# A one-layer decoder trunk on one core: residual strips turned once per feature pair, two weight sums moved to VectorE, and five joins of the last two token tiles as TensorE products

## The chip, the cores and the metric

The kernel runs on 1 core of one Trainium2 chip. The metric is the device time of one execution in microseconds; of several runs the median counts. Engines: TensorE (PE; its weight loads are listed as PEld), VectorE (DVE), ScalarE (ACT), GpSimd (POOL), and SyncE (SP), which issues most of the DMAs.

## The reference, cut to what matters

512 tokens of 2048 features, fp32, go through one layer. The change touches the feed-forward part and the end:

```python
h = h + concat([out_a, out_b]) @ w_o             # mixer, not touched
u = rmsnorm(h, ln_ffn)
gate = causal_dwconv(u @ w_gate, conv_f_w, conv_f_b)     # 2048 -> 6144, 3 taps
h = h + (gelu(gate) * (u @ w_up)) @ w_down
u = rmsnorm(h, ln_ple)
e = sigmoid(u @ w_ple_gate) * (p @ w_ple_proj)
h = h + rmsnorm(e, ln_ple_post)
out = rmsnorm(h, ln_final)
```

## The kernel before, in words

Every matrix product is done in three terms: each operand is split into a rounded high part and a low part (ScalarE writes the high part, line 138, VectorE the low part, line 139), and TensorE adds high x high, high x low and low x high. Weights come by DMA, are split by `wfill_`, and up to three split weights stand ready ahead of TensorE (`LOOK`, `HL`).

Phase 1 (to about 900 us) is the mixer. Phase 2 has four stages.

**Gate stage (about 905 to 1820 us).** `w_gate` and `w_up` are multiplied in blocks of 128 output features, with the recursion for 2x2 blocks that needs seven products instead of eight. `gate_order` lists the units: for each n from 0 to 47 (n // 2 is the pair of feature blocks, n % 2 the matrix, gate or up) the seven products `q5 p1 p4 p6 p7 p2 p3`, 336 in all, each 24 matmuls of 256 columns (lines 1302 to 1304). `unit` does one of them. Its weight operand is a sum of weight quarters, made by `gate_unit`: `q5` loads two quarters and VectorE adds them (line 1143) into the buffer `"s"`; for `p6` and `p3` GpSimd then adds another quarter into the same buffer with an accumulating DMA (line 1160). The first and last n do the `p6` sum on VectorE. The buffers are x0 to x3 for even n and x4 to x7 for odd n. The units start `p1 p4 p2` of n = 0, `p1` of n = 1, `q5 p7 p6` of n = 0, then `q5 p4` of n = 1, `p3` of n = 0, `p6 p7 p2` of n = 1, `q5` of n = 2.

After `p3` of an even n the convolution and GELU write the tile c in x9 (`conv`, lines 1346 to 1352); after `p3` of the odd n the product of both is taken (line 1433), and every second pair is spilled to DRAM (`spill`, with four subtractions on VectorE).

Beside it the residual h, 16 strips of 128 features x 512 tokens in DRAM (`hd`), is turned to token order (`hx`), for use after 2100 us: `turn` transposes 32x32 blocks on VectorE (line 1404) and stores them with four DMAs in pieces of 128 bytes (line 1407); the strip is loaded into the tile `acc` (named row in the trace) by line 1414. The program places a turn at every 18th unit.

Instructions of this stage are ordered by a scheduler: each goes when its operands are ready in the scheduler's own model, the higher priority first; weight loads and splits have a raised priority. On each engine, and in the SP queue, the order is then fixed, and each instruction waits for its turn.

**Down stage and embedding gate (about 1820 to 2497 us).** Not touched by the change.

**The end.** The last 256 gate columns are done per token tile (tt = 0 to 3, 128 tokens each), in the order written by hand on TensorE, VectorE, ScalarE and GpSimd. For each tile: 48 matmuls of 256 columns; a tanh (line 1699) and a chain of small VectorE and ScalarE operations (lines 1700 to 1705); `rstd` (line 1636) with a power on GpSimd (line 1623) gives the scale r; `joined` computes e r + h for a block of 512 columns (line 1650, four blocks a tile); `rfin` (lines 1641 to 1644) with a second power on GpSimd gives the last scale; `final` multiplies a block by it (ScalarE line 1655, VectorE line 1657) and stores it (line 1658). The join of block 3 of a tile and its four `final` blocks come after the next tile's chain.

Of the kernel before, what the change touches and what calls it, by code (L numbers as in the profile page):

```python
# [6 lines left out]
AF = mybir.ActivationFunctionType  # L7
# [6 lines left out]
KT = D // 128  # L14
# [6 lines left out]
NF = FF // 128  # L21
# [69 lines left out]
class Builder:  # L91
# [1039 lines left out]
    def gate_unit(self, n, u):  # L1131
        nc, p, w = self.nc, n // 2, n % 2
        par = 4 * w
        src = lambda i, j: self.A["wgu"][2 * p + i, w, j]
        buf = lambda i: self.t(self.bp, "x%d" % (par + i), (128, 8, 128), bufs=1)

        def load(k, i, j):
            t = buf(k)
            nc.sync.dma_start(t, src(i, j))
            return t  # L1140
        def add(o, a, b):
            with self.tc.high_priority(offset=-W['offw'] if n < 1 else 0):
                nc.vector.tensor_tensor(o, a, b, ALU.add)
            return o
        g = self.gw.setdefault(n, {})
        if u == "q5":
            g[21], g[22], g["s"] = load(0, 1, 0), load(1, 1, 1), buf(3)
            return add(g["s"], g[21], g[22])
        if u == "p1":
            g[11] = load(2, 0, 0)  # L1150
            return g[11]
        if u == "p4":
            return g[22]
        if u == "p7":
            if n < 2:
                g[11] = load(2, 0, 0)
            return add(g[21], g[21], g[11])
        if u == "p6" and n in (0, NF - 1):
            return add(g["s"], g["s"], g[11])
        nc.gpsimd.dma_start(g["s"], src(0, 0 if u == "p6" else 1), accum_op=ALU.add)  # L1160
        return g["s"]

# [68 lines left out]
    def phase2(self):  # L1231
        nc, A, k2 = self.nc, self.A, self.k2
        V, SC, G, TE = nc.vector, nc.scalar, nc.gpsimd, nc.tensor
# [5 lines left out]
        acc = self.t(self.cp, "row", (128, S + 2), bufs=1)[:, 0:S]  # L1239
        self.LOOK = 3  # L1240
        hd = [self.dp.tile([128, 2, S], F32, name="hd%d" % i) for i in range(8)]
# [52 lines left out]
        B = lambda n, shape=(128, 2, S), dt=F32: self.t(self.bp, "x%d" % n, shape, dt, bufs=1)  # L1294
# [106 lines left out]
        hx = [self.dp.tile([S, 512], F32, name="hx%d" % i) for i in range(4)]  # L1401

        def turn(m):
            V.transpose(acc, acc)
            for a in range(4):
                f = m % 4 * 128 + 32 * a
                nc.sync.dma_start(hx[m // 4][:, f:f + 32].rearrange("(b i) j -> i b j", i=32),
                                  acc[32 * a:32 * a + 32].rearrange("i (b j) -> i b j", j=32))

        raw, c = [], None  # L1410
        for k, (n, u) in enumerate(self.gate_order()):
            m = k // 18 - 1
            if 0 <= m < KT and k % 18 == 6:
                nc.sync.dma_start(acc, hd[m // 2][:, m % 2])
            if 0 <= m < KT and k % 18 == 10:
                turn(m)
            for m in late.get((n, u), ()):
                squares(m)
            unit(n, u)
            if n == 1 and u == "p6":  # L1420
                self.rstd_bcast(acc, D, RMS_EPS, k2, rs, rt)
                c = B(9)
                conv(0, o, c)
            if u != "p3":
                continue
            p, o = n // 2, G_.pop(n)["out"]
            if n == 0:
                continue
            if n % 2 == 0:
                c = B(9)  # L1430
                conv(p, o, c)
                continue
            V.tensor_tensor(o, o, c, ALU.mult)
            raw.append(o)
            if p % 2 == 1:
                spill(p // 2, raw)
                raw = []
# [3 lines left out]
        h3 = [PT[{0: 5, 1: 3, 2: 6, 3: 4}[2 * (tt // 2) + cb // 2]][cb % 2][:, tt % 2] for tt in range(4) for cb in range(4)]  # L1441
# [58 lines left out]
        def small(n):  # L1500
            nonlocal at
            at += n
            return row[:, at - n:at]
# [47 lines left out]
        for cb in (0, 2, 1, 3):  # L1551
# [5 lines left out]
            if cb == 3:  # L1557
                for k in range(2):
                    r = T("e", 2, (128, 2, S))[:, 0]
# [18 lines left out]
        MU, AD = ALU.mult, ALU.add  # L1578
        et = [self.slot(n) for n in (39, 15, 40, 41, 42, 43, 0, 1)]
        e = [et[i % 8][:, i // 8] for i in range(16)]  # L1580
# [66 lines left out]
        def joined(tt, r, cbs):  # L1647
            for cb in cbs:
                ix = tt * 4 + cb
                V.scalar_tensor_tensor(e[ix], e[ix], r, h3[ix], MU, AD)  # L1650

        def final(tt, r, cb, act=True):
            ix = tt * 4 + cb
            if act:
                SC.activation(e[ix], e[ix], AF.Copy, scale=r)
            else:
                V.tensor_scalar(e[ix], e[ix], r, None, MU)
            nc.sync.dma_start(A["out"][tt * 128:(tt + 1) * 128, cb * S:(cb + 1) * S], e[ix])

        for cb in range(4):  # L1660
# [8 lines left out]
            n, w = (8, 512) if cb < 3 else (4, 256)  # L1669
# [18 lines left out]
        with self.tc.manual_schedule(engines={ET.PE, ET.DVE, ET.Activation, ET.Pool}):  # L1688
            for tt in range(4):
                pg = {tt: self.mm()[:, 0:256]}  # L1690
                for u in range(5):
                    if u == len(us):
                        us.append(self.wnext())
                    k = 2 * u if u < 2 else 4 * u - 4
                    gate(pg, [tt], us[u:u + 1], range(k, KT), u == 0, u == 4)

                sg, ee, x = T("e", 2, (128, 2, S))[:, 0], T("e", 2, (128, 2, S))[:, 0], e[tt * 4 + 3][:, last]
                n5 = slice(tt * 5 + 4, tt * 5 + 5)
                SC.activation(sg[:, last], pg[tt], AF.Tanh, scale=rsh[:, tt:tt + 1])
                V.scalar_tensor_tensor(ee[:, last], sg[:, last], 1.0, pp[tt][:, last], AD, MU)  # L1700
                SC.activation(ee[:, last], ee[:, last], AF.Square, accum_out=ss[:, n5])
                V.scalar_tensor_tensor(x, sg[:, last], 1.0, pp[tt][:, 0:256], AD, MU)
                SC.activation(sg[:, 0:256], x, AF.Square, accum_out=sg2[:, n5])
                V.scalar_tensor_tensor(ee[:, 0:256], hq[tt // 2][:, tt % 2, 0:256], 2.0, x, MU, MU, accum_out=sb[:, n5])
                V.tensor_tensor(x, x, gfin[3][:, last], MU)
                rn = rstd(tt)
                if tt:

                    joined(tt - 1, r, (3,))
                    for cb in range(4):  # L1710
                        final(tt - 1, rf, cb)
                r = rn
                joined(tt, r, (0,))
                rf = rfin(tt, r)
                joined(tt, r, (1, 2))
            joined(3, r, (3,))
            for cb in range(4):
                final(3, rf, cb, cb < 3)

# [64 lines left out]
```

## Time and profile before

| what | us |
|---|---|
| median of 3 runs | 2527.17 |
| lowest and highest run | 2523.64, 2529.2 |
| the profiled execution | 2528.72 |
| its span, first to last instruction | 2526.9 |
| TensorE matmul busy in the span | 2473.3 |
| VectorE busy in the span | 1903.1 |

The profile is of one execution. A row of a timeline has start, duration, engine, line, operation and tiles, and in brackets the idle time of the engine before it with what ended it. In the chain of waits each piece is followed back from the end to what released it.

### The profile page before, as it was taken

How to read it: one execution, taken by the hardware profiler on the slowest of the kernel's cores; microseconds unless marked ns; L12 is line 12 of the kernel's file. 1: busy time of each engine (PE TensorE's matmuls, PEld its weight loads, DVE VectorE, ACT ScalarE, POOL GpSimd, SP SyncE). 2: the span in 40 equal slices, each digit the busy share in tenths (PEclk: the TensorE clock that was granted, in tenths of full speed). 3: DMA queues.
4: the chain of work that ended last, by engine and by line, in shares of the span. 5: the costliest groups of instructions: out<-in, count | busy, mean ns of one | idle time of the engine just before them, and what ended most of it. 6: DMA issues, size and time to landing. Idle time of an engine off the chain costs nothing.

```text
span 2526.9 us, 51719 instructions
## 1 busy us (share of the span) xinstructions
PE 2473.3 (98%) x21858; PEld 2182.3 (86%) x21858; DVE 1903.1 (75%) x2626; ACT 1250.0 (49%) x1735; POOL 220.3 (9%) x244
## 2 busy tenths in 40 slices
PE   9989999999999989999999999999999999999997
PEld 8867777777777889999999999999988888888887
DVE  5855775776585879878988888888877787896457
ACT  6563654556442545434444444444466454535345
POOL 0000100101031000000000000000000000000001
PEclk9999999999999999999999999999999999999998
DMA  7222222222342568888877777776788686853333
GB/s 260 89 78 63 88 77 65 88 81 68 102 131 93 161 198 218 203 212 221 211 196 176 204 194 193 203 196 176 213 250 234 172 264 188 254 130 117 100 92 109
DMA packets 168570, 402.17 MB, mean 159 GB/s; under 512 B 48529, under 2 KB 60817, under 8 KB 168337
## 3 DMA queue, kind: packets, MB, share of 16 engines
q1 hardware_dynamic: 133744, 307.62, 36.9%
q0 software_dynamic: 19872, 72.36, 17.3%
q10 hardware_dynamic: 14720, 18.88, 2.2%
q8 instruction: 171, 2.80, 0.5%
q14 instruction: 63, 0.51, 0.1%
HBM read 358.16 MB, written 40.63 MB: 158 GB/s over the span
## 4 chain that ended last, share of the span: by engine, by line
PE 60%; DVE 5%; DMA 3%; issue 2%; ACT 1%; POOL 0%; SPq 0%; POOLq 0%; ACTq 0%; DVEq 0%
PE mm L1304 7%; PE mm L1303 7%; PE mm L1302 7%; PE mm L1448 6%; PE mm L1447 6%; PE mm L1451 6%; PE wk L1302 3%; PE wk L1303 3%; PE wk L1304 3%; PE mm L1590 2%; PE mm L1591 2%; PE mm L1592 2%; PE mm L173 2%; PE mm L175 2%; PE mm L177 2%
## 5 line engine op out<-in xcount | busy, mean ns | idle before, releaser
L138 ACT ACTIVATE whi<-x 128x1024 fp32r<-128x1024 f32 x332 | 351.1, 1061 | 450.5 <-PE mm L1303 181.2
L139 DVE TENSOR_TENSOR wlo<-x,whi 128x1024 fp32r<-128x1024 f32 x332 | 404.7, 1219 | 120.4 <-ACT whi L138 116.5
L1302 PE MATMUL mm<-s,whi 128*128 128x256 f32 x1432 | 398.0, 278 | 4.5 <-ACT whi L138 3.6
L1304 PE MATMUL mm<-s,wlo 128*128 128x256 f32 x1432 | 398.3, 278 | 3.8 <-DVE wlo L139 3.7
L1303 PE MATMUL mm<-s,whi 128*128 128x256 f32 x1432 | 397.9, 278 | 0.0
L138 ACT ACTIVATE whi<-wraw 128x1024 fp32r<-128x1024 f32 (+1 forms) x223 | 227.0, 1018 | 341.7 <-PE mm L175 165.3
L139 DVE TENSOR_TENSOR wlo<-wraw,whi 128x1024 fp32r<-128x1024 f32 (+1 forms) x223 | 269.4, 1208 | 132.3 <-ACT whi L138 130.3
L173 PE MATMUL mm<-x,whi 128*128 128x512 f32 x832 | 332.5, 400 | 1.5 <-DVE hT L468 0.9
L177 PE MATMUL mm<-x,wlo 128*128 128x512 f32 x832 | 332.1, 399 | 0.0
L175 PE MATMUL mm<-x,whi 128*128 128x512 f32 x832 | 330.5, 397 | 0.0
L1302 PEld LDWEIGHTS mm<-s,whi 128*128 128x128 f32 x1432 | 270.6, 189 | 5.0 <-ACT whi L138 3.8
L1304 PEld LDWEIGHTS mm<-s,wlo 128*128 128x128 f32 x1432 | 270.0, 189 | 4.7 <-DVE wlo L139 4.7
L1303 PEld LDWEIGHTS mm<-s,whi 128*128 128x128 f32 x1432 | 270.1, 189 | 0.2
L1448 PE MATMUL mm<-whi,s 128*128 128x512 f32 x680 | 265.4, 390 | 0.9 <-DVE s L157 0.9
L1447 PE MATMUL mm<-whi,s 128*128 128x512 f32 x680 | 265.6, 391 | 0.0
L173 PEld LDWEIGHTS mm<-x,whi 128*128 128x128 f32 x832 | 157.1, 189 | 37.1 <-issue 2.7
L177 PEld LDWEIGHTS mm<-x,wlo 128*128 128x128 f32 x832 | 156.9, 189 | 34.0 <-issue 1.9
L175 PEld LDWEIGHTS mm<-x,whi 128*128 128x128 f32 x832 | 157.1, 189 | 33.7 <-issue 1.8
L1451 PE MATMUL mm<-wlo,s 128*128 128x512 f32 x680 | 181.3, 390 | 0.0
L1302 PE MATMUL wk<-s,whi 128*128 128x256 f32 x584 | 162.5, 278 | 2.0 <-ACT whi L138 2.0
L1304 PE MATMUL wk<-s,wlo 128*128 128x256 f32 x584 | 162.4, 278 | 0.4 <-DVE wlo L139 0.4
L1160 POOL DMA_DIRECT2D x<-wgu x94 | 82.7, 880 | 913.5 <-DVE wlo L139 663.9
(579 smaller groups left out, 5386.2 us busy)
## 6 DMA issues: line engine op xcount, KB each, us to landing
x<-wgu SPq DMA_DIRECT2D x144, 512.0 KB, 4.4
x<-wgu POOLq DMA_DIRECT2D x94, 512.0 KB, 5.7
wraw<-wz SPq DMA_DIRECT2D x80, 512.0 KB, 3.5
x<-wd SPq DMA_DIRECT2D x52, 512.0 KB, 6.0
wraw<-wgu SPq DMA_DIRECT2D x51, 512.0 KB, 4.6
x<-wd POOLq DMA_DIRECT2D x44, 512.0 KB, 6.0
wraw<-wpg SPq DMA_DIRECT2D x31, 512.0 KB, 3.5
rd<-x SPq DMA_DIRECT2D x24, 512.0 KB, 4.7
```

The lines of the kernel that those rows point to most:

```text
L138: nc.scalar.activation(hi, raw, AF.Copy)
L139: nc.vector.tensor_tensor(lo, raw, hi.bitcast(F32), ALU.subtract)
L173: nc.tensor.matmul(ps, hi[:, k, :], xh, start=first and i == 0, stop=False)
L175: nc.tensor.matmul(ps, hi[:, k, :], xl, start=False, stop=False)
L177: nc.tensor.matmul(ps, lo[:, k, :], xh, start=False, stop=last and i == n - 1)
L1160: nc.gpsimd.dma_start(g["s"], src(0, 0 if u == "p6" else 1), accum_op=ALU.add)
L1302: TE.matmul(ps, wh[:, k, :], xh, start=k == 0, stop=False)
L1303: TE.matmul(ps, wh[:, k, :], xl, start=False, stop=False)
L1304: TE.matmul(ps, wl[:, k, :], xh, start=False, stop=k == 7)
L1447: TE.matmul(ps, x[0][:, k, ts_(tt)], w[0][:, k, :], start=first and k == 0, stop=False)
L1448: TE.matmul(ps, x[1][:, k, ts_(tt)], w[0][:, k, :], start=False, stop=False)
L1451: TE.matmul(ps, x[0][:, k, ts_(tt)], w[1][:, k, :], start=False, stop=last and k == 1)
```

## The change

In the gate stage `p3` of n = 0 and `p6` of n = 1 no longer use an accumulating DMA: SP loads the quarter and VectorE adds it. `p7` of n = 1 uses the quarter that `p6` has loaded.

A turn now writes its transpose into a tile of x9, where the convolution's result lay, and not into `acc`; the next strip is loaded into `acc` right after the transpose. Turns come after the product of an odd n (n = 3, 5, ... 33), one per pair, instead of every 18th unit.

At the end, the joins of blocks 1, 2 and 3 of tile 2 and of blocks 1 and 2 of tile 3 become two TensorE products each, added up in PSUM: identity x h, and diag(r) x e, where diag(r) is the identity scaled by VectorE. Their `final` reads PSUM. The `final` of tile 3 runs in the order 0, 3, 1, 2, with 0 and 1 on ScalarE and 3 and 2 on VectorE, instead of 0, 1, 2 on ScalarE and 3 on VectorE.

```diff
@@ gate_unit
         if u == "p7":
-            if n < 2:
+            if n < 1:
                 g[11] = load(2, 0, 0)
             return add(g[21], g[21], g[11])
-        if u == "p6" and n in (0, NF - 1):
+        if u == "p6" and n in (0, 1, NF - 1):
+            if n == 1:
+                g[11] = load(2, 0, 0)
             return add(g["s"], g["s"], g[11])
+        if u == "p3" and n == 0:
+            return add(g["s"], g["s"], load(1, 0, 1))
         nc.gpsimd.dma_start(g["s"], src(0, 0 if u == "p6" else 1), accum_op=ALU.add)
@@ phase2, gate stage
         def turn(m):
-            V.transpose(acc, acc)
+            h = B(9)[:, 0]
+            V.transpose(h, acc)
+            if m + 1 < KT:
+                nc.sync.dma_start(acc, hd[(m + 1) // 2][:, (m + 1) % 2])
             for a in range(4):
                 f = m % 4 * 128 + 32 * a
                 nc.sync.dma_start(hx[m // 4][:, f:f + 32].rearrange("(b i) j -> i b j", i=32),
-                                  acc[32 * a:32 * a + 32].rearrange("i (b j) -> i b j", j=32))
+                                  h[32 * a:32 * a + 32].rearrange("i (b j) -> i b j", j=32))
...
-        for k, (n, u) in enumerate(self.gate_order()):
-            m = k // 18 - 1
-            if 0 <= m < KT and k % 18 == 6:
-                nc.sync.dma_start(acc, hd[m // 2][:, m % 2])
-            if 0 <= m < KT and k % 18 == 10:
-                turn(m)
+        for n, u in self.gate_order():
...
             if n == 1 and u == "p6":
                 self.rstd_bcast(acc, D, RMS_EPS, k2, rs, rt)
+                nc.sync.dma_start(acc, hd[0][:, 0])
...
             V.tensor_tensor(o, o, c, ALU.mult)
             raw.append(o)
+            if 0 < p <= KT:
+                turn(p - 1)
@@ phase2, the end
+        def onto(tt, cbs, stream):
+            for cb in cbs:
+                ix = tt * 4 + cb
+                if stream:
+                    sums[ix] = self.mm()
+                    TE.matmul(sums[ix], self.K("ident"), h3[ix], start=True, stop=False)
+                else:
+                    TE.matmul(sums[ix], diag[tt], e[ix], start=False, stop=True)
...
+                if tt == 3:
+                    onto(2, (1, 2, 3), True)
+                    onto(2, (1, 2, 3), False)
+                    onto(3, (1, 2), True)
...
-                    joined(tt - 1, r, (3,))
+                    if tt < 3:
+                        joined(tt - 1, r, (3,))
                     for cb in range(4):
                         final(tt - 1, rf, cb)
                 r = rn
+                if tt >= 2:
+                    V.tensor_scalar(diag[tt], self.K("ident"), r, None, MU)
                 joined(tt, r, (0,))
                 rf = rfin(tt, r)
-                joined(tt, r, (1, 2))
+                if tt < 2:
+                    joined(tt, r, (1, 2))
             joined(3, r, (3,))
-            for cb in range(4):
-                final(3, rf, cb, cb < 3)
+            onto(3, (1, 2), False)
+            for cb in (0, 3, 1, 2):
+                final(3, rf, cb, cb < 2)
```

More of the change, by code (lines that the diff above doesn't have):

```diff
@@ L1650, in joined @@
                 V.scalar_tensor_tensor(e[ix], e[ix], r, h3[ix], MU, AD)
+        sums = {}
+        diag = {tt: small(128) for tt in (2, 3)}
+        def onto(tt, cbs, stream):
[6 more added lines that the diff above has]
+                    TE.matmul(sums[ix], diag[tt], e[ix], start=False, stop=True)
         def final(tt, r, cb, act=True):
             ix = tt * 4 + cb
+            x = sums.get(ix, e[ix])
             if act:
-                SC.activation(e[ix], e[ix], AF.Copy, scale=r)
+                SC.activation(e[ix], x, AF.Copy, scale=r)
             else:
-                V.tensor_scalar(e[ix], e[ix], r, None, MU)
+                V.tensor_scalar(e[ix], x, r, None, MU)
             nc.sync.dma_start(A["out"][tt * 128:(tt + 1) * 128, cb * S:(cb + 1) * S], e[ix])
```

## The prediction

> **What bounds the kernel now.** I read the page's engine rows first, then windows by stage, then TensorE's waits, then the chain of waits and the timelines where windows lose matmuls, last the timelines of the end. All rows are of the one profiled execution.
>
> ```profile
> PE 2473.3 (98%) x21858; PEld 2182.3 (86%) x21858; DVE 1903.1 (75%) x2626; ACT 1250.0 (49%) x1735; POOL 220.3 (9%) x244
> ```
>
> TensorE is busy 98% of the span, so a change pays only where TensorE stands or runs slowly, and after its last product. Windows show where. Columns: window, length, then busy time and count of TensorE's matmuls and weight loads, VectorE, ScalarE, GpSimd; last the granted clock, DMA share and GB/s.
>
> ```profile
> 920.00:930.00 10.00, 10.00 (x89) 10.00 (x88) 3.20 (x4) 2.84 (x5) 1.86 (x2) 0.99 0.65 168
> 930.00:950.00 20.00, 15.58 (x112) 15.09 (x112) 15.98 (x21) 7.78 (x10) 3.88 (x4) 0.83 0.65 144
> 1000.00:1080.00 80.00, 80.00 (x708) 80.00 (x707) 66.05 (x77) 36.20 (x39) 7.01 (x8) 1.00 0.88 217
> 1080.00:1245.00 165.00, 161.68 (x1375) 160.57 (x1374) 138.40 (x160) 70.22 (x78) 14.92 (x17) 1.00 0.87 219
> 1180.00:1240.00 60.00, 60.00 (x512) 60.00 (x511) 53.38 (x62) 29.38 (x33) 5.24 (x6) 1.00 0.84 199
> 1300.00:1400.00 100.00, 100.00 (x885) 100.00 (x884) 85.60 (x96) 44.88 (x49) 9.30 (x11) 1.00 0.76 199
> ```
>
> Undisturbed (1300 to 1400) the gate stage does 885 matmuls in 100 us, one per 0.113 us. Between 930 and 950 it does 112 where 177 fit: 65 x 0.113 = 7.3 us lost. Between 1080 and 1245 it does 1375 where 1460 fit: 85 x 0.113 = 9.6 us lost, although busy time lacks only 3.3 us. The rest is a slower pace at full clock: 512 in 60 us is 8.53 per us, against 8.85 between 1000 and 1080 (3.6% less). It follows the stalls and lasts long. Who stalls TensorE between 860 and 1250 (total, times, longest):
>
> ```profile
> PE mm L1304 <- DVE wlo L139: 3.7, 3, 1.8
> PE mm L1302 <- ACT whi L138: 3.6, 1, 3.6
> ```
>
> It waits for split weights. The chain of waits near 930, then GpSimd's timeline, one row each of ScalarE's and TensorE's, and two of VectorE's:
>
> ```profile
> 923.65 1.23 DVE x L139
> 924.88 0.61 DVE row L1279
> 925.49 3.70 issue
> 929.19 5.49 DMA x<-wgu
> ```
> ```profile
> 919.96 1.08 POOL L1160 DMA_DIRECT2D x<-wgu  x1 [93.57 <-DVE wlo L139]
> 929.19 0.89 POOL L1160 DMA_DIRECT2D x<-wgu  x1 [8.14 <-issue]
> ```
> ```profile
> 929.01 1.06 ACT L138 ACTIVATE whi<-x 128x1024 fp32r<-128x1024 f32 x1 [4.60 <-DMA x<-wgu]
> ```
> ```profile
> 937.77 0.58 PE L1302 MATMUL mm<-s,whi 128*128 128x256 f32 x1 [3.58 <-ACT whi L138]
> ```
> ```profile
> 918.42 2.35 DVE L139 TENSOR_TENSOR wlo<-x,whi 128x1024 fp32r<-128x1024 f32 x2
> ...
> 923.65 1.23 DVE L139 TENSOR_TENSOR x<-x,x 128x1024 fp32r<-128x1024 f32 x1 [2.28 <-ACT x L138]
> ```
>
> GpSimd issues two accumulating DMAs, in the code those of (0, "p3") and (1, "p6"). The first starts at 919.96 and ScalarE gets its data at 929.01, some 9 us later. The second's destination was split by 924.9, but it starts at 929.19, when the first had landed, and takes 5.49. TensorE stands for it from 934.2 to 937.8.
>
> The other kind of stall, again by the chain of waits, and VectorE's group of the transposes between 960 and 1200 (the last numbers are its idle time before them and what ended it):
>
> ```profile
> 1070.75 4.42 DMA hx<-row
> ...
> 1075.31 7.67 DMA row<-hd
> ```
> ```profile
> L1404 DVE STREAM_TRANSPOSE row<-row 128x512 f32<-128x512 f32 x15 | 10.6, 710 | 27.6 <-DMA row<-hd 13.9 <-issue 9.1 <-DMA x<-wgu 4.5
> ```
>
> The transposed strip is stored, only then is the next strip loaded into the same tile, and VectorE, which issues in order, stands at the transpose with the next weight split behind it: 27.6 us before 15 transposes.
>
> The end, by the timelines of TensorE, VectorE, GpSimd, ScalarE and SP:
>
> ```profile
> 2510.05 0.28 PE L1592 MATMUL mm<-whi,s 128*128 128x256 f32 x1
> ```
> ```profile
> 2512.18 0.75 DVE L1650 SCALAR_TENSOR_TENSOR s<-s,row,x 128x512 f32<-128x512 f32 x1 [0.43 <-POOL row L1623]
> ...
> 2513.68 0.74 DVE L1650 SCALAR_TENSOR_TENSOR x<-x,row,x 128x512 f32<-128x512 f32 x1
> 2514.34 0.74 DVE L1650 SCALAR_TENSOR_TENSOR s<-s,row,x 128x512 f32<-128x512 f32 x1
> 2515.00 0.42 DVE L1700 SCALAR_TENSOR_TENSOR e<-e,x 128x256 f32<-128x256 f32 x1
> ...
> 2518.03 0.75 DVE L1650 SCALAR_TENSOR_TENSOR s<-s,row,x 128x512 f32<-128x512 f32 x1 [0.43 <-POOL row L1623]
> ```
> ```profile
> 2519.68 0.98 POOL L1623 TENSOR_TENSOR row<-row,mhalf 128x1 f32<-128x1 f32 x1 [1.69 <-DVE row L1644]
> ```
> ```profile
> 2520.70 1.34 ACT L1655 ACTIVATE s<-s,row 128x512 f32<-128x512 f32 x2 [1.89 <-POOL row L1623]
> 2521.94 0.71 ACT L1655 ACTIVATE x<-x,row 128x512 f32<-128x512 f32 x1
> ```
>
> TensorE is done at 2510.3, and the last 16 us are VectorE, GpSimd and ScalarE. VectorE is late: it begins token tile 3's own chain (L1700) only at 2515.00.
>
> **The change, part by part.** Durations for it: VectorE's adds, a scaled 128x128, a full-precision product (two records) from the timeline, and the landing of the strips' stores.
>
> ```profile
> L1143 DVE TENSOR_TENSOR x<-x,x x98: 1210/1219/1227, 903.0 to 1813.3; 128x1024 f32<-128x1024 f32 x98
> L741 DVE TENSOR_SCALAR bdr<-con,par x8: 246/286/287, 25.2 to 661.5; 128x128 f32<-128x128 f32 x8
> 133.80 1.02 PE L747 MATMUL wk<-rt,bdr 128*128 128x512 f32 x2
> DMA to landing us min/median/max: 1.9/4.4/9.7
> ```
>
> *Two sums by VectorE.* Two of GpSimd's accumulating DMAs go. In their place SP issues one load more ((0, "p3"), into x1), one load moves a unit earlier ((1, "p6") takes what (1, "p7") loaded), and VectorE does two adds of 1.22 us, 2.44 together. Their cover is VectorE's idle time of 920 to 930, where it is busy 3.20 of 10: it then stood behind a split whose data the first DMA had not brought. Without the DMAs (0, "p3") can be added once "s" is split for (0, "p6"), at 920.8, and (1, "p6") once split for (1, "q5"), at 924.9. With 1.2 for the add and 2.4 for the two splits it is ready near 929, and TensorE asks at 934.2. So the 7.3 us are there to win, the low clock (0.83) behind the stall among them. x1 is free for the added load early, after (0, "p4"), but the load of x1 for (2, "q5") now waits for the add near 922 and holds SP's queue that long, raw weight loads behind it; (2, "q5") is three units of 24 x 0.113 = 2.7 us after 934.2, so this is covered. Were the cover gone, the adds would cost 2.4. Bounds: +7.3 and -2.4. I take 6.3, near the upper row, since each source is early by some 5 us, and leave 1 us for VectorE's next splits, as it is busy 15.98 of 20 there.
>
> The Trainium skill, "DMA: Bandwidth & Descriptors", section "Anatomy of one DMA", fits such a DMA as 2.0 us plus bytes over 436 GB/s, which for 512 KB is an estimate of 3.2 us. The trace has 5.49 and some 9 for these two (they also add), so the measurement decides; by the page they would have come in time, the stall would not be theirs, and the sum would be 6.3 less.
>
> *Late transposes.* The next strip is loaded as soon as the transpose has read the last one, a whole turn ahead, and the transpose writes into x9, where the convolution's result lay. The work is the same: 16 transposes of 0.71 us on VectorE, 64 stores and 16 loads on SP; the load now stands ahead of its strip's four stores in SP's queue and waits for none of them. As x9 is shared, there is one turn per pair of features, 14 units x 2.7 = 38 us apart, from about 990 to 1560. The wait ahead of L1404 goes, and with it the stalls and the slow pace: up to 9.6 us. What is late next: the stores hold x9, which ScalarE's next convolution writes seven units, 19 us, later; stores land 4.4 us (at most 9.7) after issue, so this is covered unless SP is held some 10 us more. Past 1245, where VectorE is busy 86%, it gets 0.71 us in 38 more, 88%. Bounds: +9.6, and below nothing as the last rival has it. I take 8.6, near the row of 1000 to 1080 where turns ran without loss, with 1 us for a late split somewhere.
>
> *Five joins on TensorE.* VectorE loses five L1650, and TensorE gains ten full-precision products. Two records take 1.02 us to the end of the second; with 594 ns each they start 0.43 apart, so a product costs 0.87. Eight follow 2510.3 and end at 2517.3. VectorE adds two scaled identities of 0.29. The step from 2512.18 to 2515.00 loses two joins (2513.68 to 2515.00, 1.32) and gains 0.29: tile 3 starts 1.03 earlier. Its third join had filled a wait for GpSimd and saves nothing. Tile 3's first scale comes at 2517.0 instead of 2518.03, the identity takes 0.29, so GpSimd's last power starts at 2518.94 instead of 2519.68 and the final scalings at 2519.96 instead of 2520.70. The last two products end at 2517.3 + 2 x 0.87 = 2519.0, before that. Then ScalarE and VectorE scale two blocks each, not three and one: the last ends near 2521.3 instead of 2522.65, and its store follows: 1.4 us won. Bounds: at 1.02 per product without overlap ten end at 2520.5, still near the scalings, so nothing won; if all five joins counted, 5 x 0.66 = 3.3. I take 1.4, the chain's own sum.
>
> **The sum.** 6.3 + 8.6 + 1.4 = 16.3 us. The profiled execution took 2528.7 (its span is 2526.9): 2512.4. The median of the runs is 1.5 lower, 2527.2; from it 2510.9, say 2511.
>
> **The rivals.**
> 1. *The sums don't help*: the stall near 934 has another late source behind it, SP's queue, with its one load more, or VectorE. For it: VectorE is 80% busy there. Against it: its idle 6.8 us of 920 to 930. 8.6 + 1.4 won: 2517. This is also what comes out if these DMAs were never the cause, as the page's 3.2 us would have it.
> 2. *The late turns gain nothing*: another wait keeps the pace slow until 1245. For it: DMA share 0.87 there against 0.76 later. Against it: at 0.88, between 1000 and 1080, nothing is lost. 6.3 + 1.4 won: 2519.5.
> 3. *It doesn't do what it says*: both stalls move rather than go, as the new loads, stores and adds are queued in another order. For it: one wait of TensorE of 0.4 to 2 us was enough for the slow pace. Only the end is won: 2526.
> 4. *Slower*: turns delay splits where nothing stalls now. A late turn costs a stall of 1.2 us (3.7 over 3) and the slow pace until the next turn, 3.6% of 38 = 1.4: 2.6 us. From 7 of 16 turns late what is won is gone, from 9 the kernel is slower by over 0.2%; with ten late it is 2527.2 - 17.3 (the won 16.3 and the 1 us kept back) + 26 = 2536. For it: VectorE is 86% busy, and every other turn stands just ahead of the spill's four subtractions. Against it: five turns ran without loss from 1000 to 1080 though they did wait for their strips, and these don't.
>
> **How the numbers follow.** Forecast 0.42, rival 1 0.15, rival 2 0.14, rival 3 0.16, rival 4 0.13. The first three are faster by over 0.2% (5 us, about what a measurement of this kernel can tell from no change): 0.71. Rival 3 is the same, 0.16; rival 4 slower, 0.13. The range reaches down to 2504, where the upper bounds of all three terms are (7.3 + 9.6 + 3.3 = 20.2: 2507) and a little of the start of the stage with them, and up to 2528, which takes in rivals 1 to 3 and leaves out rival 4. The forecast's own range is 2507 to 2515.
>
> **What would show it.** Right: GpSimd's first accumulating DMA in the stage is (1, "p3")'s, before 935; about 177 matmuls between 930 and 950 at a clock near 1.00; no idle time of VectorE ahead of the transposes, and these 38 us apart to about 1560; 885 matmuls per 100 us from 1000 on; VectorE's last L1700 near 1 us earlier after TensorE's last gate product, and two final scalings each on ScalarE and VectorE. Wrong: stretches at 8.5 matmuls per us between 1000 and 1560, ScalarE waiting at the convolution (L1349) for a store, TensorE waiting for a split near 934, or the final scalings waiting for products.

## The result

In runs side by side the changed kernel takes 2511.85 us (median of 5, 2509.36 to 2512.75) and the kernel before 2529.20 (2523.64 to 2530.92): ratio 0.9935, 95% interval 0.9920 to 0.9949, so 16.4 us less (12.9 to 20.2); the two medians themselves are 17.35 apart. Forecast was 2511.0. The profiled executions differ by 2528.72 - 2512.22 = 16.5 us, against a sum of 16.3.

**The profile after.** First the engine row of the page, then the same windows as before with the start of the stage (900 to 930) added, and that start in the kernel before in a block of its own. Columns as above: window, length, busy time and count of TensorE's matmuls, weight loads, VectorE, ScalarE, GpSimd; clock, DMA share, GB/s.

```profile
PE 2471.0 (98%) x21878; PEld 2176.0 (87%) x21878; DVE 1905.2 (76%) x2626; ACT 1251.6 (50%) x1734; POOL 218.2 (9%) x242
```
```profile
900.00:930.00 30.00, 27.81 (x229) 26.93 (x228) 27.99 (x40) 14.64 (x23) 0.00 (x0) 1.00 0.68 248
920.00:930.00 10.00, 9.74 (x86) 9.54 (x85) 9.96 (x14) 4.48 (x7) 0.00 (x0) 1.00 0.59 198
930.00:950.00 20.00, 18.87 (x159) 18.25 (x158) 15.31 (x19) 9.91 (x11) 2.98 (x3) 1.00 0.64 150
1000.00:1080.00 80.00, 80.00 (x708) 80.00 (x708) 69.64 (x80) 37.36 (x40) 7.09 (x8) 1.00 0.80 210
1080.00:1245.00 165.00, 165.00 (x1456) 165.00 (x1456) 141.99 (x160) 79.08 (x85) 15.22 (x18) 1.00 0.81 210
1180.00:1240.00 60.00, 60.00 (x530) 60.00 (x529) 51.61 (x58) 27.19 (x31) 5.30 (x6) 1.00 0.84 215
1300.00:1400.00 100.00, 100.00 (x884) 100.00 (x884) 86.99 (x99) 47.52 (x51) 9.73 (x11) 1.00 0.82 217
```
```profile
900.00:930.00 30.00, 27.07 (x211) 26.15 (x210) 21.28 (x28) 13.32 (x21) 1.89 (x2) 0.94 0.78 258
```

TensorE is as busy as before, 98%; the engine row tells nothing of 16 us. The windows tell where they are. Between 1080 and 1245 there are 81 matmuls more (1456 against 1375), which at 0.113 us are 9.2 us, and the pace of 1180 to 1240 is back to 530 in 60 us. Between 930 and 950 there are 47 more, and between 900 and 930 another 18; together 65, or 7.3 us. The DMA share between 1180 and 1240 is 0.84 before and after, at 512 and 530 matmuls, so that share by itself did not set the pace there. Not all stalls of the start are gone: 177 would fit into 930 to 950, and 159 are there. VectorE, which was idle for 6.8 of the 10 us from 920 to 930, is now busy 9.96.

The steps in the trace: the group of the transposes with its idle time, then the same group's first and last start, then GpSimd's first accumulating DMA of the stage.

```profile
L1409 DVE STREAM_TRANSPOSE x<-row 128x512 f32<-128x512 f32 x16 | 11.3, 706 | 0.0
```
```profile
L1409 DVE STREAM_TRANSPOSE x<-row x16: 703/706/708, 991.5 to 1563.4; 128x512 f32<-128x512 f32 x16
```
```profile
934.18 1.08 POOL L1164 DMA_DIRECT2D x<-wgu  x1 [2.84 <-DVE wlo L139]
```

No idle time is left ahead of the transposes (27.6 before), and sixteen in 571.9 us are 38.1 apart. The first accumulating DMA starts at 934.18; it is that of (1, "p3").

At the end: TensorE's last gate product, ScalarE's last scaling and SP's last stores of after, then SP's of before:

```profile
2494.39 0.28 PE L1597 MATMUL mm<-whi,s 128*128 128x256 f32 x1
```
```profile
2504.31 0.67 ACT L1673 ACTIVATE s<-mm,row 128x512 f32<-128x512 f32 x1
```
```profile
2501.36 0.33 SPq L1676 DMA_DIRECT2D out<-s  x1
2504.20 0.33 SPq L1676 DMA_DIRECT2D out<-x  x1
2504.62 1.39 SPq L1676 DMA_DIRECT2D out<-s  x3
2506.10 0.49 SPq L1676 DMA_DIRECT2D out<-x  x1
```
```profile
2518.22 4.17 SPq L1658 DMA_DIRECT2D out<-s  x4
2522.67 0.83 SPq L1658 DMA_DIRECT2D out<-x  x2
```

Counted from TensorE's last gate product (2494.67; 2510.33 before) ScalarE ends 10.3 us later and not 12.3, but SP's last issue ends 11.9 later and not 13.2. Of 2.0 us won on ScalarE, 1.25 are left at SP and 0.87 at the end of the span (15.75 against 16.62). GpSimd's power for tile 3's first scale, before and after:

```profile
2517.01 0.98 POOL L1623 TENSOR_TENSOR row<-row,mhalf 128x1 f32<-128x1 f32 x1 [2.20 <-DVE row L1636]
```
```profile
2500.24 0.54 POOL L1628 TENSOR_TENSOR row<-row,mhalf 128x1 f32<-128x1 f32 x1 [1.20 <-DVE row L1641]
```

It takes 0.54 us and not 0.98: before, a join ran on VectorE beside it (2516.86 to 2517.60), and that join is now one of TensorE's.

### The profile page after: what moved, and what is told of

It reads as the page before. It is cut to its first block, busy times and chain, and to the rows that moved or that the text cites. A ratio compares the mean times of both kernels' runs of the same rounds, so it can differ in the third digit from the quotient of the medians.

```text
span 2510.4 us, 51756 instructions
## 1 busy us (share of the span) xinstructions
PE 2471.0 (98%) x21878; PEld 2176.0 (87%) x21878; DVE 1905.2 (76%) x2626; ACT 1251.6 (50%) x1734; POOL 218.2 (9%) x242
## 4 chain that ended last, share of the span: by engine, by line
PE 65%; DVE 3%; DMA 1%; ACT 1%; issue 1%; POOL 0%; ACTq 0%; POOLq 0%; DVEq 0%
PE mm L1308 8%; PE mm L1306 8%; PE mm L1307 8%; PE mm L1453 6%; PE mm L1456 6%; PE mm L1452 6%; PE wk L1306 3%; PE wk L1308 3%; PE wk L1307 3%; PE mm L1595 2%; PE mm L1596 2%; PE mm L1597 2%; PE mm L173 2%; PE mm L175 2%; PE mm L177 2%
## 5 line engine op out<-in xcount | busy, mean ns | idle before, releaser
L1306 PE MATMUL wk<-s,whi 128*128 128x256 f32 x584 | 161.4, 276 | 0.4 <-ACT whi L138 0.4
L1307 PE MATMUL wk<-s,whi 128*128 128x256 f32 x584 | 161.3, 276 | 0.0
```

Of the source, the lines that this page charges most:

```text
L1306: TE.matmul(ps, wh[:, k, :], xh, start=k == 0, stop=False)
L1307: TE.matmul(ps, wh[:, k, :], xl, start=False, stop=False)
```

## The experiments

Two marks are used below, both from VectorE's rows of the product of the two branches (`V.tensor_tensor(o, o, c, ...)`, one per pair). The *early mark* is the start of the first full pair's product after 980 us, counted from TensorE's first gate product; the *stretch* is the time from it to the eighth, seven pairs later, 267 us without loss. One row holds both ends, here of before and after:

```profile
L1433 DVE TENSOR_TENSOR x<-x,x x8: 1212/1224/1225, 996.5 to 1272.9; 128x1024 f32<-128x1024 f32 x8
```
```profile
L1436 DVE TENSOR_TENSOR x<-x,x x8: 1224/1224/1226, 989.2 to 1256.2; 128x1024 f32<-128x1024 f32 x8
```

The gate stage begins at 901.0 and 901.5, so the early mark went from 95.5 to 87.7 us and the stretch from 276.4 to 267.0. The kernels that differ in the gate stage in one table, with the time of the runs and its ratio to the kernel before on the same chip:

| kernel | accumulating DMAs at the start | turns | early mark | stretch | median us | ratio (interval) |
|---|---|---|---|---|---|---|
| before | two | dense | 95.5 | 276.4 | 2529.2 | 1 |
| after | none | one per pair | 87.7 | 267.0 | 2511.9 | 0.9935 (0.9920 to 0.9949) |
| sums alone | none | dense | 90.5 | 278.0 | 2525.2 | 0.9982 (0.9972 to 0.9993) |
| turns alone | two | one per pair | 96.4 | 266.9 | 2519.5 | 0.9956 (0.9943 to 0.9968) |
| tail alone | two | dense | 96.5 | 277.3 | 2530.6 | 0.9999 (0.9990 to 1.0007) |
| in place | two | dense | 95.7 | 279.0 | 2528.9 | 0.9999 (0.9987 to 1.0012) |
| first DMA back | one | one per pair | 93.1 | 266.9 | 2515.2 (one run) | |
| second DMA back | one | one per pair | 93.5 | 266.9 | 2516.0 (one run) | |
| strip in x9 | none | one per pair, waiting | 87.6 | 266.9 | 2510.0 | 0.9921 (0.9899 to 0.9944) |

**The parts alone.** The sums:

```diff
-            if n < 2:
+            if n < 1:
...
-        if u == "p6" and n in (0, NF - 1):
+        if u == "p6" and n in (0, 1, NF - 1):
+            if n == 1:
+                g[11] = load(2, 0, 0)
             return add(g["s"], g["s"], g[11])
+        if u == "p3" and n == 0:
+            return add(g["s"], g["s"], load(1, 0, 1))
```

> The kernel before with only the two sums given to VectorE; turns and tail as before. Theory (the three parts are independent, and the stall between 930 and 950 us came from the two serialized accumulating DMAs): 6.3 to 7.7 us less than before, ratio 0.9970 to 0.9975, about 177 - or, where the stalls of TensorE seen after the change at 930 to 939 us are the same here, about 159 - matmuls between 930 and 950, and the turns' loss between 1080 and 1245 unchanged (about 1375 matmuls in that window, shifted by the gain). Rival A (the sums alone are not enough, the early gain needed the strips' loads to leave SP's queue): below 3 us. Rival B (the slow pace between 1093 and 1243 us was a consequence of the early stall): 15 us or more.

Measured: 4.6 us less (1.8 to 7.1), under the theory's 6.3, though 173 matmuls stand between 930 and 950, near its 177. The early mark is 5.0 us earlier, and the stretch is no shorter, so rival B falls. But the mark is one of VectorE, which the dense turns hold. TensorE's own count tells more: the first 100 us after the first gate product and the next 60, with the sums alone, then the first 100 us of the changed kernel and of the one before:

```profile
898.68:998.68 100.00, 97.03 (x829) 95.59 (x828) 89.90 (x109) 49.00 (x60) 8.29 (x9) 1.00 0.79 215
998.68:1058.68 60.00, 55.13 (x471) 53.93 (x470) 43.58 (x51) 22.07 (x25) 4.44 (x5) 1.00 0.82 202
```
```profile
901.47:1001.47 100.00, 96.68 (x828) 95.45 (x827) 90.26 (x108) 49.88 (x60) 8.28 (x9) 1.00 0.73 207
```
```profile
901.01:1001.01 100.00, 92.66 (x760) 91.43 (x759) 82.97 (x100) 47.09 (x57) 10.20 (x10) 0.95 0.77 205
```

Alone the sums win 69 matmuls there, 7.8 us, as many as in the changed kernel (68), so rival A falls. Right behind it they lose most of that: 471 matmuls in 60 us, where 531 fit and where the kernel before, between 1000 and 1080, lost none. So the dense turns cost more once the early stall is gone, which fits the 4.6 us, not 7.8, that the runs are left with; the parts are not independent. That the early stall had let VectorE get ahead of TensorE would explain it; no run here shows that.

The late turns:

```diff
-            V.transpose(acc, acc)
+            h = B(9)[:, 0]
+            V.transpose(h, acc)
+            if m + 1 < KT:
+                nc.sync.dma_start(acc, hd[(m + 1) // 2][:, (m + 1) % 2])
...
+            if 0 < p <= KT:
+                turn(p - 1)
```

> The kernel before with only the late turns (next strip loaded as soon as the transpose has read the last, transpose into x9, one turn per pair of features); sums and tail as before. Theory (VectorE's wait for the strip delays weight splits): 8.6 to 9.6 us less, ratio 0.9962 to 0.9966; the stall at 934 to 938 us stays (112 matmuls in 930 to 950), and about 885 matmuls per 100 us from 1000 us on. Rival (part of the gain after 1000 us belongs to the sums, which shift the load order): under 6 us, with stretches of 8.5 matmuls per us left between 1000 and 1560.

Measured: 11.1 us less (8.1 to 14.4); the stretch is 9.5 shorter and the early mark as late as before. That is the theory's, and the loss at 930 to 950 stays (107 matmuls).

The tail:

```diff
+                if tt == 3:
+                    onto(2, (1, 2, 3), True)
+                    onto(2, (1, 2, 3), False)
+                    onto(3, (1, 2), True)
...
-            for cb in range(4):
-                final(3, rf, cb, cb < 3)
+            for cb in (0, 3, 1, 2):
+                final(3, rf, cb, cb < 2)
```

> The kernel before with only the five joins on TensorE and the final scalings shared two and two. Theory of the prediction: 1.4 us less; by the trace of the changed kernel, where the span's end came 0.9 us earlier after the last gate product: 0.9 us less, ratio 0.9996. Rival: nothing, as that 0.9 us is the spread of SP's store issues at the end; then 0.0 to 0.3 us. No difference to before until TensorE's last gate product.

Measured: nothing that the runs can tell (0.3 us less; the interval goes from 1.8 more to 2.5 less). The traces tell more: from TensorE's last gate product to the end of the span the four profiles with the old tail (before, sums, turns, in place) take 16.1 to 16.6 us, mean 16.4, and the eight with the new tail and the old order of stores 15.3 to 16.1, mean 15.6. So the tail wins 0.8 us, by profiles that spread over 0.5 us (old) and 0.8 us (new).

**What makes the turns cheap.** The theory was that VectorE's wait for the strip delays the splits. First the new place in the program without the second tile:

```diff
             V.transpose(acc, acc)
...
+            if 0 < p <= KT:
+                turn(p - 1)
+                if p < KT:
+                    nc.sync.dma_start(acc, hd[p // 2][:, p % 2])
```

> The kernel before with one turn per pair of features, as the change places them, but the transpose still in place and the next strip loaded behind its own four stores; no second tile. It tells apart what makes the turns cheap. If it is VectorE's wait for a strip, then 38 us between turns leave time enough for stores (4.4 us) and load (7.7 us) and this gains as much as the late turns with two tiles: 8.6 to 9.6 us. If it is the second tile and the load ahead of the stores that count, idle time of VectorE ahead of the transposes remains (over 10 us of 27.6 in all) and it gains under 5 us. If the turns' density alone counts, it again gains as much as with two tiles; this run and that one then differ by under 1 us, and density is left to be told from the wait by another run.

Measured: no difference to before, and not for any of the reasons given, since the turns are not 38 us apart. VectorE's transposes, grouped, and their first and last start:

```profile
L1404 DVE STREAM_TRANSPOSE row<-row 128x512 f32<-128x512 f32 x16 | 11.3, 709 | 32.8 <-DMA row<-hd 19.7 <-issue 13.1
```
```profile
L1404 DVE STREAM_TRANSPOSE row<-row x16: 702/711/714, 962.9 to 1205.7; 128x512 f32<-128x512 f32 x16
```

The turns stand as close as in the kernel before, sixteen in 243 us (there 960.2 to 1200.1): nothing ties a turn to its pair but the order of priority, and the scheduler lets each go as soon as its own chain of load, transpose and stores allows. It is the tile of x9, which the convolution holds, that spaces them. The run tells that the program place has no effect by itself; wait and density are left to the next.

```diff
-            V.transpose(h, acc)
-            if m + 1 < KT:
-                nc.sync.dma_start(acc, hd[(m + 1) // 2][:, (m + 1) % 2])
+            nc.sync.dma_start(h, hd[m // 2][:, m % 2])
+            V.transpose(h, h)
```

> The changed kernel, with the strip loaded straight into the tile of x9 that is turned (in place) and not into a tile of its own: one turn per pair as in the changed kernel, 38 us apart, but each transpose again stands behind a load that can start only when the convolution's result is used. It tells the wait from the density of the turns. If the wait is the cause: VectorE idle 15 to 40 us ahead of the 16 transposes (27.6 for 15 in the kernel before), TensorE waiting for low splits again, and some 4 to 11 us of the 11 that late turns gain are lost. If it is that turns 16 us apart were too dense: no loss (under 1.5 us), idle time or not.

Measured: 2509.96 us (2509.26 to 2511.12), no slower than the changed kernel. VectorE's transposes in it:

```profile
L1410 DVE STREAM_TRANSPOSE x<-x 128x512 f32<-128x512 f32 x16 | 11.4, 712 | 27.7 <-DMA x<-hd 27.7
```

VectorE waits 27.7 us ahead of the transposes, as long as in the kernel before (27.6), and it costs nothing: the stretch is 266.9. **The theory that the wait itself was the cause falls.** What differs is how soon the waits follow each other. VectorE's turns in the kernel before, in order of time, and two of this one:

```profile
1037.09 0.71 DVE L1404 STREAM_TRANSPOSE row<-row 128x512 f32<-128x512 f32 x1 [2.36 <-DMA row<-hd]
1055.09 0.71 DVE L1404 STREAM_TRANSPOSE row<-row 128x512 f32<-128x512 f32 x1 [4.53 <-DMA x<-wgu]
1065.58 0.71 DVE L1404 STREAM_TRANSPOSE row<-row 128x512 f32<-128x512 f32 x1 [0.43 <-DMA row<-hd]
1083.11 0.71 DVE L1404 STREAM_TRANSPOSE row<-row 128x512 f32<-128x512 f32 x1 [5.18 <-DMA row<-hd]
```
```profile
1034.68 0.71 DVE L1410 STREAM_TRANSPOSE x<-x 128x512 f32<-128x512 f32 x1 [3.28 <-DMA x<-hd]
1071.39 0.71 DVE L1410 STREAM_TRANSPOSE x<-x 128x512 f32<-128x512 f32 x1 [1.29 <-DMA x<-hd]
```

Waits and turns from 1035 to 1084 hold VectorE 12.5 + 2.8 = 15.3 us. Its other work fills some 85% of the time (86.99 of 100 between 1300 and 1400 after, less 1.9 for the turns), so in these 49 us some 7 are spare. The rest, some 8 us, is a backlog, and at 1083 TensorE stands:

```profile
1084.98 0.38 PE L1304 MATMUL mm<-s,wlo 128*128 128x256 f32 x1 [1.80 <-DVE wlo L139]
```

So the new theory is one of backlog: a hold of VectorE, whether work or wait, is free as long as the split weights ahead outlast it and spare time makes it good before the next. Two runs measure this without any strip. In the first, single holds of rising length:

```diff
+            if p in (17, 19, 21):
+                k = {17: 3, 19: 5, 21: 7}[p]
+                V.tensor_reduce(c[:, 0, 0:1], c.rearrange("p a s -> p (a s)").unsqueeze(1).broadcast_to([128, k, 1024]), mybir.AxisListType.XY, ALU.add)
```

> The changed kernel with three instructions more on VectorE, sums over the convolution's used result read 3, 5 and 7 times, after the pairs 17, 19 and 21 (near 1610, 1690 and 1760 us): they hold VectorE some 3.3, 5.4 and 7.5 us in one piece, where nothing stalls. They measure how long a hold TensorE outlives and what a late split costs. From the kernel before, where a hold of 6 us ended in a stall of 1.8: 3.3 us costs nothing, 5.4 us 0 to 1.5 us of stall, 7.5 us 2 to 4 us. Theory on the slow pace (a late low split is followed by matmuls 0.117 to 0.118 us apart and not 0.113, for tens of us): windows behind a stall show 850 per 100 us, not 885. Rival (the slow pace belonged to the stretch 1093 to 1243 us): 885 right after each stall. Rival 4 of the prediction priced such a late split at 1.2 us of stall and 1.4 of pace.

```profile
L1442 DVE TENSOR_REDUCE x<-x x3: 3347/5478/7611, 1599.7 to 1752.0; 128x1 f32<-128x3072 f32 x1, 128x1 f32<-128x5120 f32 x1, 128x1 f32<-128x7168 f32 x1
```
```profile
1700.00:1760.00 60.00, 60.00 (x531) 60.00 (x531) 53.39 (x53) 27.85 (x30) 5.33 (x6) 1.00 0.68 176
1760.00:1820.00 60.00, 59.49 (x525) 59.30 (x524) 53.70 (x62) 29.04 (x33) 4.43 (x5) 1.00 0.79 224
```

Holds of 3.35 and 5.48 us cost nothing, one of 7.61 costs some 7 matmuls (525, against 532 from 1760 to 1820 in the changed kernel), 0.8 us: less than expected. So TensorE outlives some 6.8 us here. No slow pace follows. In the second, seven holds of 5.48 us, one per n:

```diff
+            if 34 <= n <= 40 and u == "p2":
+                g = G_[n]
+                V.tensor_reduce(g["vx"][:, 0, 0:1], g["fm"].rearrange("p a s -> p (a s)").unsqueeze(1).broadcast_to([128, 10, 512]), mybir.AxisListType.XY, ALU.add)
```

> The changed kernel with seven holds of VectorE of 5.5 us each (a sum over a used tile read ten times), one per n from 34 to 40, that is 19 us apart, where nothing stalls and no DMA is waited for. The strip waits of the kernel before came every 12 to 17 us (up to 5.2 us, and 0.7 for the turn itself); with the strip in x9 waits of the same sum, 27.7 us, came every 38 us and cost nothing; a single hold of 5.5 us cost nothing and one of 7.6 cost 0.8. Theory (VectorE's backlog: a hold is made good from its spare 15%, 2.9 us in 19, and what is not made good adds up until the split weights ahead, some 6.9 us of work, are used up): no loss at the first hold, some 1.2 us at the second and 2.6 at each further one, 14 us in all; the windows behind the stalls show whether the pace is 0.118 us per matmul there. Rival (each hold stands for itself, and it was the strips' DMAs beside the weight loads that cost the time): no loss, under 1.5 us in all.

```profile
1560.00:1600.00 40.00, 40.00 (x355) 40.00 (x354) 36.28 (x38) 18.83 (x20) 3.56 (x4) 1.00 0.69 173
1600.00:1740.00 140.00, 133.11 (x1145) 132.12 (x1144) 137.93 (x126) 58.85 (x64) 12.40 (x14) 0.99 0.71 185
1740.00:1830.00 90.00, 90.00 (x766) 90.00 (x766) 74.81 (x86) 40.85 (x46) 7.11 (x8) 1.00 0.74 200
```

Measured: the gate stage is 13.9 us longer (936.4 against 922.5), the one run 13.3. The first hold is free, the stalls begin at the second (TensorE waits 0.6, 1.5, 1.5, 1.9 and 1.4 us), and VectorE is busy 137.93 of 140. So holds that are free alone cost 2 us each in a row, with no DMA waited for. Where the stalls and a short low clock are, 94 matmuls are lost, 10.6 us (1145 where 1239 fit); the other 3.4 us are a slow pace that follows the last stall to the end of the stage, at full clock and with nothing waiting (766 where 796 fit, 0.117 us each). So the sum of 14 came out by luck, not by its parts: the holds came 21 to 26 us apart and not 19, which left fewer stalls, and the pace made up for it.

**Which of the two DMAs.** The changed kernel with the first back, then with the second:

```diff
-        if u == "p3" and n == 0:
-            return add(g["s"], g["s"], load(1, 0, 1))
```

> The changed kernel with the sum of (0, "p3") made by GpSimd's accumulating DMA again; (1, "p6") stays on VectorE. Theory (two accumulating DMAs, one behind the other, were late; one alone is in time): the stall of 3.6 us at 934 us does not come back; 930 to 950 us keeps 150 or more matmuls (159 in the changed kernel, 112 in the one before) and the time is within 1.5 us of the changed kernel's 2511.9. Rival (the first DMA alone, 9 us from start to use, is the late one): 3 to 7 us more and under 130 matmuls there.

```diff
-            if n < 1:
+            if n < 2:
                 g[11] = load(2, 0, 0)
...
-        if u == "p6" and n in (0, 1, NF - 1):
-            if n == 1:
-                g[11] = load(2, 0, 0)
+        if u == "p6" and n in (0, NF - 1):
```

> The changed kernel with the sum of (1, "p6") made by GpSimd's accumulating DMA again (and (1, "p7") loading its quarter itself); (0, "p3") stays on VectorE. Theory (two in a row): this DMA now starts near 925 us, when its destination has been split, and takes 5.5; the data are split near 933, just before TensorE asks at about 934: a stall of 0 to 1 us, 150 matmuls or more in 930 to 950 us, within 1.5 us of 2511.9. Rival (this DMA is late by itself): the stall of 3.6 us with the low clock behind it is back, under 130 matmuls there, 5 to 7 us more.

Both theories miss, and the rivals hold in the main: 133 matmuls and 3.3 us more with the first DMA (the rival had under 130, and 3 to 7 us), 109 and 4.2 us with the second (under 130, and 5 to 7). The window of 930 to 950 with the first DMA, then with the second; the chain of waits of the first, and the second's landing time:

```profile
930.00:950.00 20.00, 17.13 (x133) 16.73 (x132) 16.82 (x22) 7.00 (x8) 3.81 (x4) 0.91 0.63 146
```
```profile
930.00:950.00 20.00, 14.92 (x109) 14.41 (x108) 14.29 (x16) 6.72 (x8) 3.67 (x3) 0.83 0.49 121
```
```profile
917.66 8.50 DMA x<-wgu
```
```profile
DMA to landing us min/median/max: 8.7/8.7/8.7
```

Alone, the first takes 8.5 us and the second 8.7, not 5.5; each brings most of the loss back (early mark 5.4 and 5.8 us later; the single runs 3.3 and 4.2 us longer than the changed kernel's median, and 5.2 and 6.1 longer than the 2509.96 of the strip in x9, on the same chip). They do not add up, since both feed one stall: both together cost 8.7. That one stood behind the other was not what made it. With the first alone TensorE does not even stand for that DMA's data, but 2.75 us for a low split that VectorE reaches late, after it had stood 2.6 us for the DMA.

**Two tries at more.** The order of SP's last stores, and the late adds of squares:

```diff
-        with self.tc.manual_schedule(engines={ET.PE, ET.DVE, ET.Activation, ET.Pool}):
+        with self.tc.manual_schedule(engines={ET.PE, ET.DVE, ET.Activation, ET.Pool, ET.SP}):
...
-            for cb in (0, 3, 1, 2):
+            for cb in (3, 0, 2, 1):
```

> The changed kernel with SP's last stores in the order in which their blocks become ready (tile 2's block 3 ahead of tile 3's blocks; 3, 0, 2, 1 in tile 3). In the changed kernel's trace five stores are issued one after the other from 2504.20 to 2506.59, the first of them behind a block that was ready 2.3 us later than tile 2's last. Theory: one store fewer is left at the end, and the span ends 0.5 to 0.9 us earlier after TensorE's last gate product (15.75 us in the changed kernel), ratio to the changed kernel 0.9997. Rival: what lands last, not what is issued last, sets the end; then 0.0 to 0.2. The runs' own spread hides either; the trace tells.

Measured: 2510.46 us (2509.47 to 2512.61), ratio to before 0.9927 (0.9914 to 0.9939), not to be told from the changed kernel's by the runs. SP's last stores in it:

```profile
2502.17 0.91 SPq L1676 DMA_DIRECT2D out<-s  x2
2505.01 0.33 SPq L1676 DMA_DIRECT2D out<-x  x1
2505.43 0.38 SPq L1676 DMA_DIRECT2D out<-s  x1
2505.91 0.40 SPq L1676 DMA_DIRECT2D out<-x  x1
2506.40 0.40 SPq L1676 DMA_DIRECT2D out<-s  x1
```

Tile 2's last store now leaves with the one at 2502.17, and four, not five, are left for the end. The span ends 14.9 us after the last gate product here and 15.1 in the run with both tries: 0.6 under the mean of 15.6 with the old order. By the two traces the theory holds.

```diff
-                V.tensor_tensor(acc, acc, sq, ALU.add)
+                (V if m < 8 else G).tensor_tensor(acc, acc, sq, ALU.add)
```

> The changed kernel with the eight late adds of squares (line 1283, 0.69 us each, 911 to 927 us) given from VectorE to GpSimd, which stands idle then. TensorE's stalls that are left after the change (5 us between 906 and 940) stand where VectorE is busy 9.96 of 10 us. Theory: with 5.5 us of work fewer on VectorE the low splits come earlier, and 2 to 4 us are won. Rival: GpSimd takes 1.3 to 1.7 us for such an add, and the chain of eight squares and adds makes the norm's scale late, for which TensorE's broadcast product and the first convolution wait: nothing won or up to 3 us lost.

> The changed kernel with both: SP's last stores in order, and the late adds of squares on GpSimd. The two touch places 1560 us apart, so the gains should add: 2.5 to 4.9 us less than the changed kernel by the theories of the two, 2507 to 2509.5 us; 2511.9 or more if both rivals hold.

Measured: 2516.55 us (ratio to before 0.9949, 0.9937 to 0.9962) and 2514.73 (0.9939, 0.9926 to 0.9953) with both: slower than the changed kernel's by 4.7 and 2.9. Against the run with the stores alone (2510.46, side by side with these two on one chip) they are 6.1 and 4.3 longer, so the adds cost more than the rival had it. The loss is at the start (early mark 92.5 and 92.6 us, 87.6 with the stores alone), but not where the rival had it. ScalarE writes each square into one tile and stands behind GpSimd's add with the next weight split queued after it. ScalarE, TensorE, GpSimd and VectorE of the run with the adds alone:

```profile
911.18 0.63 ACT L1282 ACTIVATE rsa<-hT 128x512 f32<-128x512 f32 x1 [3.10 <-POOL row L1283]
```
```profile
917.59 0.58 PE L1306 MATMUL wk<-s,whi 128*128 128x256 f32 x1 [3.65 <-ACT whi L138]
```
```profile
916.67 1.47 POOL L1283 TENSOR_TENSOR row<-row,rsa 128x512 f32<-128x512 f32 x1 [0.74 <-ACT rsa L1282]
918.88 1.47 POOL L1283 TENSOR_TENSOR row<-row,rsa 128x512 f32<-128x512 f32 x1 [0.74 <-ACT rsa L1282]
```
```profile
917.57 1.65 DVE L139 TENSOR_TENSOR wlo<-x,whi 128x1024 fp32r<-128x1024 f32 x1 [0.56 <-ACT whi L138]
919.78 1.66 DVE L139 TENSOR_TENSOR wlo<-x,whi 128x1024 fp32r<-128x1024 f32 x1 [0.56 <-ACT whi L138]
```

TensorE waits 3.65 us for a high split. VectorE does not win its 5.5 us either: a split of 1.22 us that begins during an add of GpSimd takes 1.65, and ends 1.08 and 1.09 us after GpSimd's, as if it began only then.

## Why the prediction was right, step by step

- **What bounds.** Right: what was won is where TensorE stood or ran slowly, at a share of 98% before and after.
- **Two sums, 6.3 us.** Under-sized: the early mark is 7.8 us earlier. Its parts came out otherwise: between 930 and 950 only 47 of the 65 matmuls are won, 5.3 us and not 7.3, since 159 stand there and not 177; another 18 are won before 930, where I had counted nothing. The cause was named rightly, with two steps wrong. I put the second DMA's lateness down to its standing behind the first, and alone it is slow too, since whichever goes first is (8.5 and 8.7 us). And of VectorE's 6.8 idle us between 920 and 930 the DMA made only 4.6: the other 2.28 ended with ScalarE's split of 922.55, which had waited for TensorE. Rivals 1 and 3, no gain here, fall. The fit of the Trainium skill ("DMA: Bandwidth & Descriptors", "Anatomy of one DMA"), by my estimate 3.2 us for 512 KB, does not describe these DMAs: 8.5 and 8.7, and none of the stage under 5.1 in any trace.
- **Late turns, 8.6 us.** Right in size (9.4 on the stretch, so rival 2 falls), in the spacing by x9, and in what the trace shows; the reason was half right. I had the 27.6 us of waiting as such be the cost. As much waiting, 27.7 us, once per pair, cost nothing. The step that failed is "The wait ahead of L1404 goes, and with it the stalls and the slow pace": the stalls go because the holds are 38 us and not 16 apart, and VectorE's spare time covers each. That is shown for the stalls (strip in x9; seven holds). They are the smaller part: of the 9.6 us, TensorE stands 3.3, and 6.3 are the slow pace, which goes away with the dense turns; how they make it stays open. With the sums alone it is the other way round: of the 6.8 us lost in the 60 us shown above, TensorE stands 4.9. The load ahead of the stores is a reserve that the time does not show.
- **The tail, 1.4 us.** Over-sized: 0.8 by twelve profiles, not measurable by the runs. The steps up to the scalings came out or better (tile 3's chain 1.1 us earlier after the last gate product, for 1.03; ScalarE's last scaling 2.0, for 1.35). I had the third join of tile 2 "saves nothing", as it filled a wait for GpSimd; without it beside, GpSimd's power takes 0.54 us and not 0.98, in each of the ten profiles with the new tail. "And its store follows" did not come out. SP's order was fixed with tile 2's last store behind a block of tile 3, and five stores of 0.3 to 0.5 us stood in line. In the order in which blocks are ready, the tail's gain is 1.4, by two profiles.
- **The sum.** The two traces give 7.8 + 9.4 + 0.9 = 18.1; off it go 0.9 us by which the down stage was longer (470.7 against 469.8; 469.3 to 470.6 in the eight other profiles of the changed kernel and its variants), 0.5 by which the gate stage began later, and 0.2 in the embedding gate: 16.5. That the sum met the median to 1 us is in part luck: two terms were too small, the tail too large, and what went off was in no term.
- **Rival 4** priced a late turn at 2.6 us each. A hold of 5.5 us alone costs nothing, and sixteen turns that waited for their strips cost nothing at 38 us apart, so ten late turns would hardly have made the kernel slower. A price of that kind (2 us each in the run of seven) fits only holds closer than VectorE can make good.

## What to carry to other kernels

An engine that works ahead of the bound has a budget: how much prepared work lies ahead, and how much spare time it has between two delays. A wait within that budget is free however large the sum of such waits looks, so read in the profile how far apart the waits are before pricing them, and spread them before removing them. And when an operation at the end gets earlier, check the queue through which its result leaves.

## What the runs showed of the hardware that was not expected

- **Two paces at full clock.** Matmuls come 0.113 us apart, or 0.117 to 0.118, for as long as 90 us, with a granted clock of 1.00 and no wait (1740 to 1830 in the run with seven holds). Its long stretches began behind a stall, but not behind each: of that run's five stalls one was followed by it. Short ones need none: the first 45 gate products of the kernel before (901.0 to 906.2) come 0.118 us apart, ahead of the first stall of the stage. What sets it is open.
- **Accumulating DMAs** of 512 KB land in a median of 5.8 us over the stage in the changed kernel (5.2 to 8.7). The first one of the stage was slow in each of the 14 profiles, whichever sum it served: 9.0 us before, 8.5 and 8.7 with one of the two back, 7.4 after, 7.1 to 9.5 in all, and 5.2 to 6.6 for the one behind it. It is not alone: 22 of the changed kernel's other 91 take over 7 too. Why is open.
- **A busy GpSimd slows VectorE**, and the reverse: GpSimd's adds of one size took 1.28 to 2.99 us in the run with the adds alone (its spans are rough), and its power at the end 0.54 or 0.98, without and with a join on VectorE. The Trainium skill, "SBUF — State Buffer", section "SBUF: two separate sides", has the two share a port pair that one instruction holds to its end, also against VectorE operations with two inputs in SBUF; the ends some 1.1 us after GpSimd's agree with it.
- **Steadiness.** The kernel before spread over 12 us in 29 runs on one chip (2523.67 to 2535.67), the one with the strip in x9 over 1.9 in 4 and the changed one over 3.4 in 5, though fewer runs spread less by chance alone. What the dense turns lose differs from run to run: between 1080 and 1245 the four profiles with dense turns have 1353 to 1397 matmuls.
